# Attention loop of a windowed-attention and Fourier encoder: products in 64 rows of the TensorE array, two side by side

## The chip, the cores and the metric

One core of a Trainium2 chip runs the whole program. The metric is the device time of one execution in microseconds. Five engines work beside each other, each through its own queue of instructions: TensorE (PE: matrix products out of SBUF into the eight banks of PSUM), VectorE (DVE), ScalarE (ACT), GpSimd (POOL) and SyncE (SP, which here only issues DMAs). They meet at semaphores. A product of TensorE can use all 128 rows of its array (128 values of the summed dimension) or one half of them, rows 0 to 63 or 64 to 127; two products in different halves can run at the same time.

## The reference, cut to what matters

Two sequences (2048 and 512 tokens, 1024 channels) go through an attention layer and a Fourier layer. The change is in the attention layer, which is, for 16 query heads of 64 channels and 4 key heads, in blocks of 128 queries against up to 384 keys:

```python
h = rmsnorm(x, g)
z = h @ w_in                              # q, k, v, gate
scores = q . k * 64**-0.5 + bias          # a block and its two neighbours
m = max(scores, sink)
p = exp(scores - m)
p = p / (sum(p) + exp(sink - m))
o = p @ v
x = x + (o * silu(gate)) @ w_out
```

All matrix products have operands split into a high and a low part, so that each is three products: high x high, high x low, low x high (`matmul3`, line 114).

## The kernel before

**Chunks, turns, units.** The tokens are worked on in five chunks of 512 (line 37): chunk 0 is the short sequence, chunks 1 to 4 the long one. For a chunk, keys and values are projected first (`kv_proj`), then a loop of 17 turns (n = 0 to 16) does the attention: turn n computes scores and probabilities of one pair of heads for two blocks of queries (`new`, called `one` and `two`), and transposes and value products of those of the turn before (`old`). A block on the edge of a sequence has two key blocks (256 wide), the others three (384 wide): in chunk 0 one of each two blocks is narrow, in chunks 1 and 4 one of each four.

**What fills TensorE.** Into the turns the projections of q and gate of later head pairs are laid, and at the end those of the output. One unit is one step of 128 summed channels: three products of 512 columns, 8 units to a projection. A fixed list of quotas says how many units stand before and behind the value products, about four each.

**A turn on the engines.** TensorE: scores of both blocks (`scores`, L530), in 64 rows, since a head has 64 channels, the two heads side by side; transposes of the probabilities of the turn before (`transp`, L589), also in 64 rows; four units (L117) in 128 rows; value products (`av`, L615) in 128 rows; four units. VectorE adds the bias to the scores and takes the minimum of the negated ones (`biased`, L549), ScalarE takes the exponentials (`exps`, L557), VectorE inverts the sums and divides (`divide`, L565 and L569; one of four divisions on ScalarE, L567). `parts` (L597, L598) splits the transposed probabilities: ScalarE casts the high part out of PSUM, VectorE subtracts for the low one. `out_evac` takes the values out: copy `t2` on ScalarE (L624), two adds on VectorE (L633), then the gate on GpSimd and another split. `evac_q` and `evac_g` take a finished projection out (L465, L466; L473, L475), in chunk 0 with a scaling on VectorE ahead.

**Order.** Each engine works in the order in which the program is written (`seq` and `pe` chain the instructions), and waits where a semaphore is not there yet. Bias rows and weights come by DMA issued from SP; in chunk 0 the weights are split into high and low there (`load_w`, a cast of 1024 columns on ScalarE, four subtractions on GpSimd). `extra` lays side work into the turns: squares for the norms of the next chunk (L193) and sums and splits of the next layer's weights (L722, L778).

**PSUM.** Four banks (`psum`, buffers taken in turn by projections, transposes and value products) and four for scores (`spt`), of which the transposes of the second block also use one.

## Time and profile before

| | us |
|---|---|
| median of three runs | 1571.45 (1568.65 to 1572.51) |
| span of the profiled execution | 1566.4 |
| attention loop, chunk 0, window 41.3 to 174 | 132.4 TensorE busy of 132.7 |
| attention loop, chunk 2, window 459 to 603 | 144.0 TensorE busy of 144.0; VectorE 115.7, ScalarE 102.3, GpSimd 43.6 |

The span runs from the first to the last instruction that the profiler saw. "Busy" counts a product from its start to its modelled end; products overlap in the array, so that a TensorE that is always busy can still lose time between them, and the distance from start to start tells what a product really takes. In a group row the columns are line, engine, operation, output and inputs, shape, count, then busy time, mean ns of one, and idle time before them with what ended it. In a timeline row they are start and length in us, then the same; idle time before it stands in brackets. Of `64*128` and `128*128` the first number is the rows of the array.

### The profile page before, as it was taken

The numbers are of one execution on the slowest core, as the hardware profiler recorded it, in microseconds if no ns is written. First come the engines' busy times: TensorE is split into PE (matmuls) and PEld (weight loads), VectorE is DVE, ScalarE is ACT, GpSimd is POOL, SyncE is SP. The second block draws the span as 40 slices with busy tenths as digits, with TensorE's granted clock in tenths as the row PEclk, the third lists the DMA queues.
The fourth block names the chain that finished last, engine by engine and source line by source line (L and its number), as shares of the span: only waits on it lengthen the run. The fifth ranks groups of instructions, "written<-read, shape, count | busy, mean of one in ns | idle before, by whom it ended". The sixth has DMA issues, their size and how long they took to land.

```text
span 1566.4 us, 27701 instructions
## 1 busy us (share of the span) xinstructions
PE 1555.5 (99%) x9818; PEld 1306.6 (83%) x9818; DVE 1178.3 (75%) x2843; ACT 877.1 (56%) x2120; POOL 446.7 (29%) x614
## 2 busy tenths in 40 slices
PE   9999999999999999999999999999999999999998
PEld 7888888888898888988888888888888888888886
DVE  5888555887548886378873588767999888989886
ACT  7788534676237774256761476636556564333353
POOL 2575642421403413124224142123121211101100
PEclk9999999999999999999999999999999999999999
DMA  8588696665865576756749665675675569656852
GB/s 295 203 330 297 222 369 208 214 242 202 294 228 196 207 267 231 245 190 234 267 150 322 239 235 196 227 258 203 217 249 189 195 243 399 210 202 250 296 193 95
DMA packets 100423, 372.34 MB, mean 238 GB/s; under 512 B 11204, under 2 KB 22220, under 8 KB 82877
## 3 DMA queue, kind: packets, MB, share of 16 engines
q1 hardware_dynamic: 82716, 297.38, 54.2%
q0 software_dynamic: 16400, 70.04, 11.5%
q10 hardware_dynamic: 1168, 3.15, 0.6%
q8 instruction: 78, 1.28, 0.3%
q14 instruction: 61, 0.49, 0.1%
HBM read 280.06 MB, written 90.47 MB: 237 GB/s over the span
## 4 chain that ended last, share of the span: by engine, by line
PE 92%; DVE 3%; issue 2%; DMA 1%; POOL 0%; ACT 0%; SPq 0%; POOLq 0%; DVEq 0%; ACTq 0%
PE gp L117 15%; PE qp L117 14%; PE spt L117 11%; PE op L117 7%; PE av L615 6%; PE spt L530 6%; PE W L117 5%; PE fo L117 5%; PE vp L117 3%; PE Wo L117 3%; PE Z L117 3%; PE pt L589 3%; PE Zo L117 2%; PE z L1166 2%; PE ABp L117 1%
## 5 line engine op out<-in xcount | busy, mean ns | idle before, releaser
L117 PE MATMUL gp<-h,wg 128*128 128x512 f32 x960 | 237.8, 396 | 0.0
L117 PE MATMUL qp<-h,wq 128*128 128x512 f32 x960 | 237.1, 396 | 0.0
L549 DVE CUSTOM_DVE_ANT_0 S<-spt,b 128x385 f32<-128x385 f32 (+1 forms) x320 | 161.0, 529 | 98.9 <-PE spt L530 62.4
L117 PEld LDWEIGHTS gp<-h,wg 128*128 128x128 f32 x960 | 174.9, 188 | 37.3 <-issue 1.0
L117 PEld LDWEIGHTS qp<-h,wq 128*128 128x128 f32 x960 | 174.9, 188 | 36.5 <-issue 0.3
L557 ACT ACTIVATE S<-S 128x385 f32<-128x385 f32 (+1 forms) x320 | 190.7, 610 | 15.7 <-DVE S L549 15.7
L597 ACT CAST pts<-pt 128x384 fp32r<-128x384 f32 (+1 forms) x240 | 95.1, 462 | 179.3 <-PE pt L589 176.5
L598 DVE TENSOR_TENSOR pts<-pt,pts 128x384 fp32r<-128x384 f32 (+1 forms) x240 | 112.5, 519 | 22.4 <-ACT pts L597 22.2
L639 POOL TENSOR_TENSOR uT<-o,uT 128x256 fp32r<-128x256 f32 x75 | 55.5, 740 | 234.2 <-ACT uT L638 234.1
L117 PE MATMUL spt<-wo,uT 128*128 128x512 f32 x480 | 120.3, 391 | 0.0
L117 PE MATMUL op<-wo,uT 128*128 128x512 f32 x480 | 118.9, 391 | 0.0
L615 PEld LDWEIGHTS av<-pts,v 128*128 128x128 f32 x576 | 101.4, 188 | 18.8
L615 PE MATMUL av<-pts,v 128*128 128x512 f32 (+1 forms) x576 | 115.7, 341 | 0.0
L117 PE MATMUL fo<-wo,tTu 128*128 128x512 f32 x480 | 115.0, 392 | 0.0
L569 DVE TENSOR_SCALAR S<-S 128x384 f32<-128x384 f32 (+1 forms) x192 | 103.2, 537 | 6.8
L117 PEld LDWEIGHTS op<-wo,uT 128*128 128x128 f32 x480 | 89.4, 188 | 18.5
L117 PEld LDWEIGHTS spt<-wo,uT 128*128 128x128 f32 x480 | 89.1, 188 | 18.3
L530 PE MATMUL spt<-kwin,qab 64*128 64x384 f32 (+1 forms) x960 | 104.1, 343 | 0.0
L117 PEld LDWEIGHTS fo<-wo,tTu 128*128 128x128 f32 x480 | 88.3, 188 | 17.3
L530 PEld LDWEIGHTS spt<-kwin,qab 64*128 64x128 f32 x960 | 75.5, 184 | 28.2 <-issue 25.0
L635 POOL TENSOR_TENSOR o<-o,s 128x256 f32<-128x256 f32 x75 | 55.1, 735 | 129.4 <-DVE o L633 128.6
L589 PEld LDWEIGHTS pt<-ident,S 64*128 64x128 f32 x1328 | 69.8, 138 | 4.4 <-issue 1.8
(342 smaller groups left out, 3207.3 us busy)
## 6 DMA issues: line engine op xcount, KB each, us to landing
wo<-wsd SPq DMA_DIRECT2D x32, 1024.0 KB, 6.5
wq<-wsd SPq DMA_DIRECT2D x31, 1024.0 KB, 7.7
wg<-wsd SPq DMA_DIRECT2D x31, 1024.0 KB, 6.3
x<-x1d SPq DMA_DIRECT2D x40, 512.0 KB, 3.5
b<-b21d SPq DMA_DIRECT2D x40, 512.0 KB, 4.6
b<-rowd SPq DMA_DIRECT2D x40, 384.0 KB, 4.4
xs<-in_x_dram SPq DMA_DIRECT2D x23, 512.0 KB, 6.6
s2d<-gt POOLq DMA_DIRECT2D x40, 256.0 KB, 4.3
```

The lines of the kernel that those rows point to most:

```text
L117: ins = pe(PE.matmul(out, a[i], b[j], start=start and i + j == 0, stop=stop and i == 1, skip_group_check=more))
L530: pe(PE.matmul(banks[j][:, 2 + k0 * P : 2 + k1 * P], res["q"][rows, qp, b * P : (b + 1) * P], kwin[g][rows, kp, b * P + k0 * P : b * P + k ...
L549: seq(DVE, DVE.tensor_tensor_reduce(out=s[:, e0:e1], in0=ps[:, 1 + e0 : 1 + e1], in1=st["bias"][:, j, 386 - e1 : 386 - e0][:, ::-1], scale ...
L557: last_exp[0] = seq(ACT, ACT.activation(s[:, e0:e1], s[:, e0:e1], AF.Exp, bias=s[:, 386:387], scale=-1.0, accum_out=s[:, 387:388]))
L569: seq(DVE, DVE.tensor_scalar(s[:, ks], s[:, ks], den, None, ALU.mult))
L589: pe(PE.transpose(ps[h][:, kb, j, :], ss[j][rows, 1 + kb * P : 1 + (kb + 1) * P], ident[rows, rows]))
L597: seq(ACT, ACT.copy(hi, ps[:, k0:k1]))
L598: seq(DVE, DVE.tensor_tensor(lo, ps[:, k0:k1], f32(hi), ALU.subtract))
L615: pe(PE.matmul(to, v, pt, start=n == part == 0, stop=part == 1 and n in (1, len(todo) - 1), skip_group_check=n > 1,))
L635: eng.tensor_tensor(o, o, s, ALU.mult)
L639: low = eng.tensor_tensor(lo, o, f32(hi), ALU.subtract)
L1166: PE.matmul(to, m[part][:, g * P : (g + 1) * P], ch[:, 0, :, odd * P : (odd + 1) * P], start=part == 0, stop=part == 1,)
```

## The change

Every projection and score bank is now a PSUM tile with a fixed place: four for projections (`pj`), two for scores (`spt`), and two (`tv`) that transposes and value products share. In the loop every unit is laid beside a unit of another projection (`beside`): the one takes rows 0 to 63 of its operands, the other rows 64 to 127 of its own, and later the halves change places. The value products of two blocks run side by side in the same way, in two halves with a unit between them. Where a bank is to be written from the other half of the array, TensorE first waits until its last product into that bank is done (`swapped`). The turn is written anew: scores of the second block stand behind both transposes, and the values of a turn are taken out behind the first scores of the next. The transposes that spread the norms of the next chunk are in 64 rows too. Outside the loop projections stay whole (`whole`). The columns of all products together stay the same.

```diff
-    banks = [pstack.enter_context(tc.tile_pool(name="psum", bufs=4, space=PSUM))]
+    banks = []
+    psum = pstack.enter_context(tc.tile_pool(name="psum", bufs=1, space=PSUM))
+    pj = [psum.tile([P, 512], F32, name=f"pj{i}") for i in range(4)]
+    spsum = pstack.enter_context(tc.tile_pool(name="spsum", bufs=1, space=PSUM))
+    spt = [spsum.tile([P, 512], F32, name=f"spt{i}") for i in range(2)]
+    tv = spsum.tile([P, 2, 512], F32, name="tv")
+    spt += [tv[:, 0], tv[:, 1]]
...
+            class Product:
+
+                def __init__(self, place, left, right):
+                    self.ps, self.left, self.right, self.done, self.last = place, left, right, 0, [None, None]
...
+                def whole(self, k):
+                    first = self.done == 0
+                    self.done += 6
+                    matmul3(self.ps, self.left(k), self.right(k), first, self.done == 6 * KD, True)
...
+            def beside(*pairs):
+
+                swapped([(unit[0].last, h) for pair in pairs for h, unit in enumerate(pair) if unit is not None])
+                for upper, lower in pairs:
+                    both = []
+                    for h, unit in enumerate((upper, lower)):
+                        if unit is not None:
+                            both.append((unit[0], h) + unit[0].parts(unit[1], slice(64 * h, 64 * h + 64)))
+                    for i, j in ((0, 0), (0, 1), (1, 0)):
+                        for out, h, a, b in both:
+                            out.last[h] = pe(PE.matmul(out.ps, a[i], b[j], **out.flags()))
+
+            def swapped(places):
+
+                before = []
+                for last, h in places:
+                    if last[1 - h] is not None:
+                        before.append(last[1 - h])
+                        last[1 - h] = None
+                if before:
+                    wait = pe(PE.nop())
+                    for ins in before:
+                        tc.add_manual_dep(wait.ins, ins.ins.name, DONE, reason="other rows of a bank")
...
+                    products, last = [], [[None, None], [None, None]]
+                    for i in range(2):
+                        gb, k0, k1 = span(b + i)
+                        for kb in range(k0, k1):
+                            v = vblk[gb - 1 + kb][:, g].rearrange("p a d -> p (a d)")
+                            for part in range(2):
+                                pt = pts[:, part, i, kb].rearrange("p h q -> p (h q)")
+                                products.append((i, v, pt))
+                    by_block = [[m for m in products if m[0] == i] for i in range(2)]
+
+                    def half(swap):
+                        todo = by_block[::-1] if swap else by_block
+                        if swap:
+                            swapped([(last[1], 0), (last[0], 1)])
+                        for n in range(max(map(len, todo))):
+                            for h in range(2):
+                                if n < len(todo[h]):
+                                    i, v, pt = todo[h][n]
+                                    rows = slice(64 * h, 64 * h + 64)
+                                    last[i][h] = pe(PE.matmul(
+                                        tv[:, i, :256], v[rows], pt[rows], start=not swap and n == 0,
+                                        stop=swap and n == len(todo[h]) - 1, skip_group_check=True,
+                                    ))
...
-                    work += steps
+                fetches, loads, o, evacs = zip(*(qg_proj(c, i, hs, res[i // 2], invb0) for i in range(16)))
+                load_op, op_tiles, op = out_proj(c, uTs)
+                loads += tuple(lambda m=m: load_op(0, m) for m in range(4))
...
+                for k in range(KD):
+                    o[0].whole(k)
+                evacs[0]()
+                loads[2]()
+                loads[3]()
+                loads[4]()
+                for k in range(4):
+                    o[1].whole(k)
+                four = range(4)
...
+                def fills(n):
+
+                    t0, t1, t2, t3 = op_tiles
+                    if n < 14:
+                        x, y, z = (o + (t3,))[n + 1 : n + 4]
+                        return [((y, k), (x, 4 + k)) for k in four], [((y, 4 + k), (z, k)) for k in four]
...
+                    first, second = fills(n)
+                    if n == 0:
+                        beside(*(((o[1], 4 + k), (o[2], k)) for k in four))
                     if new:
...
-                        new[0].scores(one, spt[:2])
-                        if c:
-                            new[0].scores(two, spt[2:])
+                        new[0].scores(one)
+                    split = out_evac() if out_evac else None
+                    if new:
                         for j in range(2):
                             new[0].biased(one, j)
+                        new[0].exps(one, 0)
+                    beside(*first[:1])
                     if old:
                         old[0].transp(older[0], 0)
-                    if new and not c:
-                        new[0].scores(two, spt[2:])
+                        old[0].parts(older[0])
+                    if new:
+                        new[0].exps(one, 1)
...
+                    beside(*first[1:])
+                    if new:
+                        new[0].divide(one, 0, False)
+                        new[0].divide(one, 1, on_act == one)
...
-                    ahead_j = 2 if n == 15 else 1 if c and old else 0
                     if new:
-                        for j in range(ahead_j):
-                            new[0].biased(two, j)
+                        new[0].scores(two)
...
+                    if n < 15:
+                        evacs[n + 1]()
+                        loads[n + 5]()
                     if old:
-                        for b in older:
-                            old[0].parts(b)
+                        old[0].parts(older[1])
                     if new:
                         for j in range(2):
-                            new[0].exps(one, j)
-                    if split and c:
-                        split()
-                        split = None
...
-                        for j in range(ahead_j, 2):
                             new[0].biased(two, j)
...
-                        new[0].divide(one, 0, False)
...
-                        new[0].divide(one, 1, on_act == one)
...
-                    for i in range(quota[2 * n] if n < 15 else 18 - n):
-                        (work or op).pop(0)()
...
+                    beside(*second[:2])
                     if old:
-                        old[0].av(old[1])
-                        split = old[0].out_evac(old[1])
+                        halves = old[0].av(old[1])
+                        halves[0]()
+                    beside(*second[2:3])
+                    if old:
+                        halves[1]()
+                        out_evac = lambda old=old: old[0].out_evac(old[1])
+                    beside(*second[3:])
...
+                out_evac()()
```

**TensorE around the value products** (chunk 2, head pair 3; `q`/`g` for the projections of pair 4, `pts` the split probabilities). Before: four units, the value products, the next projection.

```order
L117 MATMUL qp2_4_6395<-h2_6_5138,wq2_4_6154 128x512 x3
L117 MATMUL qp2_4_6395<-h2_7_5146,wq2_4_6154 128x512 x3
L615 MATMUL av2_3_0_6497<-pts2_3_0_6428,v1_4_3036 128x512 x2
L615 MATMUL av2_3_0_6497<-pts2_3_0_6428,v2_5_5500 128x512 x2
L615 MATMUL av2_3_0_6497<-pts2_3_0_6428,v1_3_3008 128x256 x2
L615 MATMUL av2_3_0_6497<-pts2_3_0_6428,v2_6_5503 128x256 x2
L117 MATMUL gp2_4_6515<-h2_0_5088,wg2_4_6156 128x512 x3
L117 MATMUL gp2_4_6515<-h2_1_5097,wg2_4_6156 128x512 x3
```

Now: the last of six pairs of the first half, one unit of two projections side by side, and the first of the second half.

```order
L661 MATMUL tv_81<-pts2_3_0_7878,v2_6_6687 128x256
L661 MATMUL tv_81<-pts2_3_0_7878,v2_5_6684 128x256
L661 MATMUL tv_81<-pts2_3_0_7878,v2_6_6687 128x256
L484 MATMUL pj1_73<-h2_6_6311,wg2_4_7453 128x512
L484 MATMUL pj2_74<-h2_2_6278,wq2_5_7613 128x512
L484 MATMUL pj1_73<-h2_6_6311,wg2_4_7453 128x512
L484 MATMUL pj2_74<-h2_2_6278,wq2_5_7613 128x512
L484 MATMUL pj1_73<-h2_6_6311,wg2_4_7453 128x512
L484 MATMUL pj2_74<-h2_2_6278,wq2_5_7613 128x512
L661 MATMUL tv_81<-pts2_3_0_7878,v1_4_3618 128x256
L661 MATMUL tv_81<-pts2_3_0_7878,v1_3_3591 128x256
L661 MATMUL tv_81<-pts2_3_0_7878,v1_4_3618 128x256
```

The value products went from eight in 128 rows to two halves of 64 rows, with a unit between them.

**ScalarE, one turn** (head pair 4, first two blocks `S2_4_0` and `S2_4_1`; `t22_3_0` and `uT2_3` are values of pair 3, `th2_4` a gate). Before, from one copy `t2` to the next:

```order
L624 COPY t22_3_0_6506<-av2_3_0_6497 64x512
L510 COPY b2_4_6282<-sk_308 128x2x2
L597 CAST pts2_3_2_6547<-pt2_3_2_0_6548 128x6x64
L597 CAST pts2_3_2_6547<-pt2_3_2_1_6549 128x6x64
L597 CAST pts2_3_2_6547<-pt2_3_3_0_6562 128x6x64
L597 CAST pts2_3_2_6547<-spt0_233 128x6x64
L557 ACTIVATE S2_4_0_0_6543<-S2_4_0_0_6543 128x385
L557 ACTIVATE S2_4_0_1_6545<-S2_4_0_1_6545 128x385
L638 CAST uT2_3_6031<-o2_3_0_6508 128x256
L557 ACTIVATE S2_4_1_0_6575<-S2_4_1_0_6575 128x385
L557 ACTIVATE S2_4_1_1_6589<-S2_4_1_1_6589 128x385
L567 ACTIVATE S2_4_0_1_6545<-S2_4_0_1_6545 128x384
```

Now, the same stretch:

```order
L672 COPY t22_3_0_8018<-tv_81 64x512
L598 ACTIVATE S2_4_0_0_8024<-S2_4_0_0_8024 128x385
L636 CAST pts2_3_2_8036<-tv_81 128x6x64 x2
L598 ACTIVATE S2_4_0_1_8026<-S2_4_0_1_8026 128x385
L685 CAST uT2_3_7364<-o2_3_0_8020 128x256
L608 ACTIVATE S2_4_0_1_8026<-S2_4_0_1_8026 128x384
L527 ACTIVATE th2_4_8096<-pj1_73 128x512
L636 CAST pts2_3_2_8036<-tv_81 128x6x64 x2
L598 ACTIVATE S2_4_1_0_8106<-S2_4_1_0_8106 128x385
L598 ACTIVATE S2_4_1_1_8108<-S2_4_1_1_8108 128x385
```

The casts of the transposes stood together ahead of all exponentials; now the first two stand behind the first exponential, and the last two behind a division and the evacuation of a projection.

**VectorE, the same turn** from the adds of the values on. Before:

```order
L633 TENSOR_TENSOR o2_3_0_6508<-av2_3_0_6497,t22_3_0_6506 64x256 x2
L549 ISA S2_4_0_0_6543<-spt0_233,b2_4_6282 128x385
L549 ISA S2_4_0_0_6543 128x1
L549 ISA S2_4_0_1_6545<-spt1_234,b2_4_6282 128x385
L549 ISA S2_4_0_1_6545 128x1
L549 ISA S2_4_1_0_6575<-spt2_235,b2_4_6282 128x385
L549 ISA S2_4_1_0_6575 128x1
L598 TENSOR_TENSOR pts2_3_2_6547<-pt2_3_2_0_6548,pts2_3_2_6547 128x6x64
L598 TENSOR_TENSOR pts2_3_2_6547<-pt2_3_2_1_6549,pts2_3_2_6547 128x6x64
L598 TENSOR_TENSOR pts2_3_2_6547<-pt2_3_3_0_6562,pts2_3_2_6547 128x6x64
L598 TENSOR_TENSOR pts2_3_2_6547<-spt0_233,pts2_3_2_6547 128x6x64
```

Now:

```order
L680 TENSOR_TENSOR o2_3_0_8020<-tv_81,t22_3_0_8018 64x256 x2
L590 ISA S2_4_0_0_8024<-spt0_79,b2_4_7689 128x385
L590 ISA S2_4_0_0_8024 128x1
L590 ISA S2_4_0_1_8026<-spt1_80,b2_4_7689 128x385
L590 ISA S2_4_0_1_8026 128x1
L637 TENSOR_TENSOR pts2_3_2_8036<-tv_81,pts2_3_2_8036 128x6x64 x2
L606 RECIPROCAL S2_4_0_0_8024<-S2_4_0_0_8024 128x1
L610 TENSOR_SCALAR S2_4_0_0_8024<-S2_4_0_0_8024 128x384
L606 RECIPROCAL S2_4_0_1_8026<-S2_4_0_1_8026 128x1
L529 SCALAR_TENSOR_TENSOR s2_4_8098<-th2_4_8096,pj1_73 128x512
L637 TENSOR_TENSOR pts2_3_2_8036<-tv_81,pts2_3_2_8036 128x6x64 x2
```

The four subtractions (`pts`) stood together behind three biased scores; now two stand behind two biased scores, and the other two behind reciprocals, a division and the evacuation of the gate.

More of the change, by code (lines that the diff above doesn't have):

```diff
@@ L330, in bias_rows @@
                 return rowd, sk
-            spt = []
-            for i in range(4):
-                spt.append(spsum.tile([P, 512], F32, name=f"spt{i}"))
             def zeros(s):
@@ L381, in cols @@
                     return h[0][:, c0 : c0 + n], h[1][:, c0 : c0 + n]
-                kps = [spt[1 + t][:, :n] for t in range(2)]
+                kps = [(pj if c else spt)[1 + t][:, :n] for t in range(2)]
                 for k in range(KD):
@@ L410, in kv_proj @@
                     group = blocks[i0 : i0 + 4]
-                    ps = [bank(f"vp{c}_{i0}_{i}")[:, :256] for i in range(1 if norms else 0, len(group))]
                     if norms:
-                        ps.insert(0, spt[3][:, :256])
+                        ps = [t[:, :256] for t in spt[3:] + pj[1:]]
+                    else:
+                        ps = [t[:, :256] for t in (pj[2:3] if i0 else spt)]
                     for k in range(KD):
@@ L476, in evac_g @@
                     res["s"] = s
[L478 to L488 removed]
+                return fetch, load, out, evac_g if i % 2 else evac_q
             def attention(c, p, res, uTs):
@@ L536, in scores @@
                             ))
-                    for j in range(2):
-                        st["ps", b, j] = banks[j]
                 def edges(b):
```

215 lines of the change are left out of this document (94 added, 121 removed).

## The prediction

> **What bounds the kernel now.** First the page's busy times and its chain of work that ended last.
>
> ```profile
> PE 1555.5 (99%) x9818; PEld 1306.6 (83%) x9818; DVE 1178.3 (75%) x2843; ACT 877.1 (56%) x2120; POOL 446.7 (29%) x614
> PE 92%; DVE 3%; issue 2%; DMA 1%; POOL 0%; ACT 0%; SPq 0%; POOLq 0%; DVEq 0%; ACTq 0%
> ```
>
> TensorE works 99% of the span and carries 92% of the chain; VectorE and ScalarE have room on average. So I read TensorE's timeline of the attention loop next (chunk 2, two turns; a row is start, length, engine, line, tile, count).
>
> ```profile
> 502.71 1.33 PE L530 MATMUL spt<-kwin,qab 64*128 64x384 f32 x12
> 503.88 0.58 PE L589 MATMUL pt<-ident,S 64*128 64x64 f32 x13
> ...
> 504.71 3.03 PE L117 MATMUL qp<-h,wq 128*128 128x512 f32 x12
> 507.57 1.54 PE L615 MATMUL av<-pts,v 128*128 128x512 f32 x8
> 508.95 2.91 PE L117 MATMUL gp<-h,wg 128*128 128x512 f32 x12
> 511.79 1.33 PE L530 MATMUL spt<-kwin,qab 64*128 64x384 f32 x12
> ...
> 520.94 1.32 PE L530 MATMUL spt<-kwin,qab 64*128 64x384 f32 x12
> ```
>
> From score block to score block a turn takes 9.08 and 9.15 us, 9.12 on average. The rows follow each other without a hole: here TensorE waits for nobody. For the price of a product I take the output projection, where only 128-row products run.
>
> ```profile
> 405.67 2.88 PE L117 MATMUL op<-wo,uT 128*128 128x512 f32 x12
> 408.39 0.84 PE L117 MATMUL spt<-wo,uT 128*128 128x512 f32 x3
> ```
>
> Twelve take 2.72 us from start to start, 0.227 each. In the loop the twelve before the scores take 2.84 (508.95 to 511.79) and the twelve behind the transposes 2.86 (504.71 to 507.57): 0.12 and 0.14 more. The scores take 1.17 for six pairs; at 384/512 of 0.227 a pair they would take 1.02: 0.15 more. So one visit to the 64-row form costs **0.41 us**, and a turn is 8.71 us of work plus that.
>
> **The change, part by part.**
>
> *Visits removed.* With every product, transpose and value product of the loop in 64 rows, a chunk has one visit where it had 17 (turns 0 to 16): 16 x 5 chunks x 0.41 = 33 us less, if nothing else stopped TensorE.
>
> *Pairs in place of whole products.* A pair of 64-row products has the columns of one whole product. Not in the trace at 512 wide; nearest are the score pairs, 1.17/6 = 0.195 with both drains, 0.170 without, exactly the whole product's rate. Bounds: 0.227 (full overlap) and 0.454 (none, 24 x 0.227 = 5.4 us more a turn). I take 0.227, the rate of the score pairs; the far end contradicts that row and stays out of the range. The value product becomes 12 pairs of 256 columns. Before it was four of 512 and four of 256 in 1.38 us (507.57 to 508.95): 1.38 - 4 x 0.227 = 0.47, 0.118 for one of 256, and 12 x 0.118 = 1.41. No difference worth a term.
>
> *Two new waits of TensorE on itself in a turn* (before a bank takes products of the other rows). Between the product waited for and the wait stand six score products (0.51 us) or six projection products (0.68). Bounds: nothing, and a drain like that above, 0.2 each. I take nothing, since the work between outlasts one whole product:
>
> ```profile
> L117 PE MATMUL qp<-h,wq 128*128 128x512 f32 x960 | 237.1, 396 | 0.0
> ```
>
> 0.40 us from its start to its end; the rest is a rival below.
>
> *The moved hand-overs.* This decides. Transposes and value products now share two banks, and the values are copied out only after the next turn's first scores. By the changed order ScalarE runs: copy t, exp, two casts, exp, cast uT, division, evacuation of q or g, two casts, two exps; VectorE: two adds, two biased scores, two subtractions, reciprocal, division, reciprocal, evacuation, two subtractions, then the second block. The first value product stands behind the last subtraction, and the next copy t behind the last value product: a closed circle, once a turn. Its operations, in the trace before:
>
> ```profile
> 513.52 1.25 ACT L597 CAST pts<-pt 128x384 fp32r<-128x384 f32 x3 [3.02 <-PE pt L589]
> 514.64 0.51 ACT L597 CAST pts<-spt 128x384 fp32r<-128x384 f32 x1
> 515.01 0.65 ACT L557 ACTIVATE S<-S 128x385 f32<-128x385 f32 x1
> ...
> 515.62 0.64 ACT L557 ACTIVATE S<-S 128x385 f32<-128x385 f32 x1
> ...
> 517.82 0.61 ACT L567 ACTIVATE S<-S 128x384 f32<-128x384 f32 x1
> 518.33 0.58 ACT L473 ACTIVATE th<-gp 128x512 f32<-128x512 f32 x1
> 518.93 0.58 ACT L624 COPY t<-av 64x512 f32<-64x512 f32 x1
> ```
>
> ```profile
> 514.28 0.55 DVE L549 CUSTOM_DVE_ANT_0 S<-spt,b 128x385 f32<-128x385 f32 x1
> 514.76 0.08 DVE L549 DVE_READ_ACCUMULATOR2_ANT S<- 128x1 f32 x1
> 514.76 1.48 DVE L598 TENSOR_TENSOR pts<-pt,pts 128x384 fp32r<-128x384 f32 x3
> 516.16 0.54 DVE L598 TENSOR_TENSOR pts<-spt,pts 128x384 fp32r<-128x384 f32 x1
> ...
> 517.10 0.15 DVE L565 RECIPROCAL S<-S 128x1 f32<-128x1 f32 x1
> 517.28 0.42 DVE L569 TENSOR_SCALAR S<-S 128x384 f32<-128x384 f32 x1
> 517.62 0.22 DVE L565 RECIPROCAL S<-S 128x1 f32<-128x1 f32 x2
> ...
> 519.01 0.69 DVE L475 SCALAR_TENSOR_TENSOR s<-th,gp 128x512 f32<-128x512 f32 x1 [0.19 <-ACT th L473]
> 519.62 0.85 DVE L633 TENSOR_TENSOR o<-av,t 64x256 f32<-64x256 f32 x2
> ```
>
> An operation followed by one of its own engine is priced from start to start, one that is waited for by its length. Copy t 0.58; two adds 0.85; biased score 0.48 and its read 0.08; exp 0.61 (515.01 to 515.62); cast 0.51; two subtractions 0.47 each (a third of 514.76 to 516.16); reciprocal 0.18; division 0.34 (517.28 to 517.62); reciprocal 0.15; division on ScalarE 0.51; evacuation 0.58 there and 0.61 on VectorE; subtractions 0.47 and 0.54. Sum 7.43. Hand-overs: ScalarE to VectorE shows 0.10 (518.91 to 519.01) and occurs so twice where two semaphores are waited for; six more I estimate at 0.05: 0.50. TensorE from there: weights of the first pair 0.12 (as after a visit), six pairs 0.71, three projection pairs 0.68, five pairs 0.59 and the last one's length, 0.28 by the group of 256-wide value products:
>
> ```profile
> L615 PE MATMUL av<-pts,v 128*128 128x256 f32 x52 | 8.3, 282 | 0.0
> ```
>
> 2.38 in all. **The circle is 10.3 us**, longer than the 8.71 of work: TensorE idles 1.6 us a turn, mainly ahead of the value products, and a turn grows by 10.3 - 9.12 = 1.2. Ends: 10.1 with hand-overs of 0.03; 10.7 when the division runs 0.76 as it does beside GpSimd. Before, the casts and subtractions had no exp, division or evacuation between them, so no such circle filled a turn.
>
> *The other chunks.* In chunks 1 and 4 every other turn has a 256-wide first block, and the turn is shorter (two turns between these rows, 8.85 each):
>
> ```profile
> 265.59 1.14 PE L530 MATMUL spt<-kwin,qab 64*128 64x256 f32 x12
> 283.27 1.15 PE L530 MATMUL spt<-kwin,qab 64*128 64x256 f32 x12
> ```
>
> Narrow biased scores, exps, casts and subtractions are some 0.13 shorter each,
>
> ```profile
> L549 DVE CUSTOM_DVE_ANT_0 S<-spt,b 128x385 f32<-128x385 f32 x25 | 12.9, 552 | 0.0
> L549 DVE CUSTOM_DVE_ANT_0 S<-spt,b 128x257 f32<-128x257 f32 x24 | 9.3, 425 | 4.1 <-PE spt L530 2.5 <-issue 0.5 <-ACT b L510 0.4
> ```
>
> and three of them stand in an average circle: 9.9, +1.05. In chunk 0 six are narrow, but the cast of the next weights now stands between ScalarE's division and evacuation:
>
> ```profile
> 98.97 0.65 ACT L597 CAST pts<-pt 128x256 fp32r<-128x256 f32 x2 [1.39 <-PE pt L589]
> 99.50 1.06 ACT L145 CAST wq<-w32q 128x1024 fp32r<-128x1024 f32 x1
> 100.45 0.49 ACT L597 CAST pts<-pt 128x384 fp32r<-128x384 f32 x1
> ...
> 107.54 0.65 ACT L597 CAST pts<-pt 128x256 fp32r<-128x256 f32 x2
> ```
>
> 10.3 - 0.8 + 0.95 = 10.45, against 8.57 (98.97 to 107.54): +1.9.
>
> *Sum over 14 turns a chunk (1 to 14):* 14 x 1.9 + 28 x 1.05 + 28 x 1.2 = 27 + 29 + 34 = 90. Turn 0 has no values and turn 15 no evacuation (1.2 less, about even). Turn 16 has transposes and values with only six projection pairs: the value product's end, copy and adds (0.28 + 0.05 + 0.58 + 0.10 + 0.85 + 0.05 + 0.12 = 2.0) have two pairs of units, 1.4, beside them; casts and subtractions of a block (0.20 + 0.37 + 0.51 + 0.05 + 0.54 + 0.17 = 1.85, where 0.20 ends the transposes and 0.17 restarts TensorE) have 0.68 beside the first block and 1.36 beside the second. That stops TensorE 0.6 + 1.2 + 0.5 = 2.3 us, less the drains 1.9: 9 over five chunks. Squares (1.06 us) and splits of the next layer's weights (1.14 for two) now precede copy t on ScalarE:
>
> ```profile
> L193 ACT ACTIVATE xs<-xs 128x1024 f32<-128x1024 f32 x5 | 5.3, 1055 | 0.0
> ```
>
> ScalarE ends its second exp some 0.7 before copy t is due, so two squares in a turn cost 1.4, one 0.35, two splits 0.4. Chunks 1 to 3 have five squares (two, two and one to a turn), chunks 1 to 4 three turns with two splits: 3 x 3.2 + 12 x 0.4 = 15. Weights are fetched one at a time, two turns ahead: nothing. The Fourier phase is unchanged. Total 90 + 9 + 15 = 114 us, for a span of 1566.4 + 114 = 1680; the median, 1571.45, lies 5 us above the span: **1685**.
>
> **The rivals.**
>
> *Faster: the hand-overs stay hidden.* If ScalarE and VectorE delivered within TensorE's 8.71 us, only the drains would count: 1571 - 33 = **1538**. It decides at a circle of 8.7, 1.6 below the rows' sum; it needs an engine to take a ready operation ahead of a waiting one. For it speaks that both engines' sums (VectorE 75%) fit the turn; against it that each link is a measured length in one queue. [...]
>
> *No change: drains come back as waits.* If each self-wait cost 0.2, 2 x 0.2 x 80 = 32 would return the 33: **1571**, with the circle hidden. [...]
>
> *Half hidden:* a circle of 9.5 (0.8 less than the sum) would give 75 turns x 0.4 and the 9: about **1610**.
>
> **How the numbers follow.** Forecast 0.83; half hidden 0.05; no change 0.03; faster 0.09. The forecast's own range: below, 70 turns x 0.2 (the circle at 10.1), no cost of squares and splits (15) and none of turn 16 (9) make 1647, and as much again as the 0.2 for links shorter than their means 1633; above, 70 x 0.4 (the division beside GpSimd) and some 12 for chunk 0's fuller ScalarE make 1725. With 1630 to 1725 about 0.8 is inside, so no other case has to be. 0.3% is about what a measurement of this kernel can tell from no change. Faster 0.09, same 0.03, slower 0.88.
>
> **What would show it.** TensorE's timeline: turns of 10.3 us in chunks 2 and 3; a hole of 1 to 1.6 us ahead of the first value product, released by VectorE's subtraction; TensorE's busy share down to some 93%; no 0.12 gap between scores, transposes and projections; pairs at 0.227. Wrong if turns are near 8.7, if the holes stand at the self-waits, or if pairs take far more than 0.23.

## The result, and the profile after

| | before | after |
|---|---|---|
| median of the runs | 1571.6 us (1568.7 to 1572.5) | 1816.4 us (1811.6 to 1820.1) |
| span of the profiled execution | 1566.4 us | 1814.5 us |
| a quiet turn of chunk 2 (no square, split or transfer delays it) | 9.12 us | 11.66 us (the first two 11.51) |

The change makes the kernel slower by a ratio of 1.1563 (95% interval 1.1541 to 1.1586): 245 us where 113 were forecast. The direction was right, the size was less than half of it. The page of after, busy times and chain:

```profile
PE 1608.7 (89%) x13123; PEld 1333.5 (73%) x13123; DVE 1193.3 (66%) x2823; ACT 912.9 (50%) x2120; POOL 444.3 (24%) x614
...
PE 38%; DVE 24%; ACT 19%; issue 6%; DMA 5%; POOL 2%; SPq 0%; DVEq 0%; POOLq 0%; ACTq 0%
```

TensorE carried 92% of the chain and carries 38% now; VectorE and ScalarE work little longer than before (1193 and 913 us against 1178 and 877), but 43% of the chain runs through them. They are not full; they are waited for. TensorE's timeline of a turn of chunk 2 (projections left out) shows where:

```profile
620.47 0.68 PE L574 MATMUL spt<-kwin,qab 64*128 64x384 f32 x6
621.70 0.55 PE L627 MATMUL tv<-ident,S 64*128 64x64 f32 x12
625.11 0.59 PE L627 MATMUL tv<-ident,S 64*128 64x64 f32 x12 [0.74 <-DVE pts L637]
625.51 0.78 PE L574 MATMUL spt<-kwin,qab 64*128 64x384 f32 x6
629.21 0.97 PE L661 MATMUL tv<-pts,v 64*128 64x256 f32 x12 [1.53 <-DVE pts L637]
630.72 0.88 PE L661 MATMUL tv<-pts,v 64*128 64x256 f32 x12
632.13 0.34 PE L574 MATMUL spt<-kwin,qab 64*128 64x384 f32 x2
```

The turn takes 632.13 - 620.47 = 11.66 us, and the hole forecast ahead of the first value product is there (1.53 us, released by VectorE's subtraction). A second one, 0.74, stands ahead of the second transposes, released by the same line. ScalarE's and VectorE's casts and subtractions of this turn:

```profile
622.88 0.48 ACT L636 CAST pts<-tv 128x384 fp32r<-128x384 f32 x1
623.99 0.48 ACT L636 CAST pts<-tv 128x384 fp32r<-128x384 f32 x1 [0.62 <-DVE pts L637]
...
626.69 0.47 ACT L636 CAST pts<-tv 128x384 fp32r<-128x384 f32 x1
628.08 0.48 ACT L636 CAST pts<-tv 128x384 fp32r<-128x384 f32 x1 [0.92 <-DVE pts L637]
```

```profile
623.40 0.56 DVE L637 TENSOR_TENSOR pts<-tv,pts 128x384 fp32r<-128x384 f32 x1 [0.73 <-ACT pts L636]
624.50 0.56 DVE L637 TENSOR_TENSOR pts<-tv,pts 128x384 fp32r<-128x384 f32 x1 [0.55 <-ACT pts L636]
...
627.50 0.55 DVE L637 TENSOR_TENSOR pts<-tv,pts 128x384 fp32r<-128x384 f32 x1
628.60 0.56 DVE L637 TENSOR_TENSOR pts<-tv,pts 128x384 fp32r<-128x384 f32 x1 [0.55 <-ACT pts L636]
```

Read the two together: cast, subtraction, cast, subtraction, each waiting for the other engine. The second cast of a block, whose bank TensorE had filled by 622.25 (621.70 + 0.55), is released by the subtraction of the first head (0.62 and 0.92 us idle). In the sum of the prediction the second cast ran beside the first subtraction, as it did before. The groups over the whole kernel say the same:

```profile
L637 DVE TENSOR_TENSOR pts<-tv,pts 128x384 fp32r<-128x384 f32 (+1 forms) x320 | 169.3, 529 | 144.3 <-ACT pts L636 144.3
L661 PE MATMUL tv<-pts,v 64*128 64x256 f32 x1792 | 155.5, 296 | 114.1 <-DVE pts L637 114.1
...
L636 ACT CAST pts<-tv 128x384 fp32r<-128x384 f32 (+1 forms) x320 | 145.9, 456 | 126.6 <-DVE pts L637 115.3
```

The program has this wait in it. These are the casts of one turn in ScalarE's order with what they wait for, two blocks of two heads, first of after, then of the experiment "one link" below, in which the second head has another bank:

```
L636 CAST pts_3_2_8036<-tv 128x6x64 [waits PE_49,Activation_49]
L636 CAST pts_3_2_8036<-tv 128x6x64 [waits DVE_49]
L636 CAST pts_3_2_8036<-tv 128x6x64 [waits PE_49]
L636 CAST pts_3_2_8036<-tv 128x6x64 [waits DVE_49]
```

```
L636 CAST pts_3_2_8036<-tv 128x6x64 [waits PE_49,Activation_49]
L636 CAST pts_3_2_8036<-pj_72 128x6x64 [waits PE_49]
L636 CAST pts_3_2_8036<-tv 128x6x64 [waits PE_49]
L636 CAST pts_3_2_8036<-pj_72 128x6x64 [waits PE_49]
```

In after both heads' transposes lie in two banks of one tile (`tv`), and ScalarE's read of the second bank is ordered behind VectorE's read of the first. The traces agree: there the second cast of a block idles 0.62 and 0.92 us for VectorE, in "one link" it starts 0.38 behind the first (593.86 to 594.24) with no wait.

### The profile page after: what moved, and what is told of

It is laid out like the page before. It is cut to its first block, busy times and chain, and to the rows that moved or that the text cites. A ratio compares the mean times of both kernels' runs of the same rounds, so it can differ in the third digit from the quotient of the medians.

```text
span 1814.5 us, 34001 instructions
## 1 busy us (share of the span) xinstructions
PE 1608.7 (89%) x13123; PEld 1333.5 (73%) x13123; DVE 1193.3 (66%) x2823; ACT 912.9 (50%) x2120; POOL 444.3 (24%) x614
## 4 chain that ended last, share of the span: by engine, by line
PE 38%; DVE 24%; ACT 19%; issue 6%; DMA 5%; POOL 2%; SPq 0%; DVEq 0%; POOLq 0%; ACTq 0%
DVE pts L637 8%; ACT pts L636 6%; PE pj L124 5%; PE W L124 4%; ACT S L598 4%; PE pj L484 3%; PE tv L661 3%; PE spt L124 3%; DVE S L590 3%; PE tv L124 3%; PE Wo L124 3%; DVE o L680 3%; PE fo L124 2%; PE Z L124 2%; ACT t L672 2%
## 5 line engine op out<-in xcount | busy, mean ns | idle before, releaser
L484 PE MATMUL pj<-h,wg 64*128 64x512 f32 x1800 | 490.8, 402 | 0.0
L484 PE MATMUL pj<-h,wq 64*128 64x512 f32 x1680 | 455.8, 400 | 0.0
L484 PEld LDWEIGHTS pj<-h,wg 64*128 64x128 f32 x1800 | 324.5, 190 | 19.1 <-issue 1.8
L484 PEld LDWEIGHTS pj<-h,wq 64*128 64x128 f32 x1680 | 301.5, 189 | 17.7
L637 DVE TENSOR_TENSOR pts<-tv,pts 128x384 fp32r<-128x384 f32 (+1 forms) x320 | 169.3, 529 | 144.3 <-ACT pts L636 144.3
L661 PE MATMUL tv<-pts,v 64*128 64x256 f32 x1792 | 155.5, 296 | 114.1 <-DVE pts L637 114.1
L661 PEld LDWEIGHTS tv<-pts,v 64*128 64x128 f32 x1792 | 136.8, 194 | 155.6 <-DVE pts L637 148.6
L636 ACT CAST pts<-tv 128x384 fp32r<-128x384 f32 (+1 forms) x320 | 145.9, 456 | 126.6 <-DVE pts L637 115.3
L627 PE MATMUL tv<-ident,S 64*128 64x64 f32 x1792 | 90.0, 231 | 75.7 <-DVE pts L637 38.9
L484 PE MATMUL pj<-wo,uT 64*128 64x512 f32 x660 | 111.8, 402 | 0.0
```

Source lines behind the costliest of these rows:

```text
L484: out.last[h] = pe(PE.matmul(out.ps, a[i], b[j], **out.flags()))
L627: pe(PE.transpose(ps[h][:, kb, j, :], ss[j][rows, 1 + kb * P : 1 + (kb + 1) * P], ident[rows, rows]))
L636: seq(ACT, ACT.copy(hi, ps[:, k0:k1]))
L637: seq(DVE, DVE.tensor_tensor(lo, ps[:, k0:k1], f32(hi), ALU.subtract))
L661: last[i][h] = pe(PE.matmul(tv[:, i, :256], v[rows], pt[rows], start=not swap and n == 0, stop=swap and n == len(todo[h]) - 1, skip_group_ ...
```

## The experiments

Theory T: a turn is one closed circle of hand-overs between the three engines, as forecast, with one link more than the sum had. Rivals: R1, the 64-row products and TensorE's waits on itself; R2, the place of evacuation and weight load in the queues. Theory D came later, for chunk 0.

**Two tiles.** The shared tile becomes two, so the copy of the values is cut in two and the adds in four.

```diff
-    tv = spsum.tile([P, 2, 512], F32, name="tv")
+    tv = [spsum.tile([P, 512], F32, name=f"tv{i}") for i in range(2)]
...
-                    last_evac[0] = seq(ACT, ACT.copy(t2, ps[64:128]))
+                    for i in range(2):
+                        last_evac[0] = seq(ACT, ACT.copy(t2[:, i], ps[i][64:128]))
```

> The two banks for transposes and values become two tiles of one bank each; the copy of the values becomes two copies, the two adds four. Theory T (a turn is one closed circle of hand-overs between ScalarE, VectorE and TensorE, in which the second cast of a block also waits for the first subtraction because both read one tile): a cast and two hand-overs, some 0.65 us, leave the circle twice a turn, the extra copy and adds put 0.4 back: turns of chunk 2 from 11.66 to about 10.7, casts wait for TensorE only, time about 1745. Rival R1 (the 64-row products and TensorE's waits on itself cost the time): no change or a little more, 1816 to 1830. Rival R2 (the time comes from the evacuation of the projections and the weight casts standing between the two blocks in the queues): no gain either, 1816 to 1830.

Measured 1736.1 us (one run); quiet turns of chunk 2 mostly 10.49. Both are near T's numbers (1745 and 10.7), and both rivals fall.

**Evacuation late, and both edits together.**

```diff
+                    if old:
+                        old[0].parts(older[1])
                     if n < 15:
                         evacs[n + 1]()
                         loads[n + 5]()
-                    if old:
-                        old[0].parts(older[1])
```

> The evacuation of the next projection and the load of weights stand behind the casts and subtractions of the second block, nothing else is changed. Theory T: 0.58 on ScalarE and 0.61 on VectorE leave the circle: turns of chunk 2 from 11.66 to about 10.4; in chunk 0 the weight cast (1.05) and the scaling (0.69) leave it as well, 2.9 a turn at most; time about 1705. The interlock of the casts stays in view (each second cast released by VectorE's subtraction). Rival R1 (TensorE's own side): 1816. Rival R2 (it is the place of these steps and nothing else): turns near 9.1 and a time near 1580.

> Both edits: two tiles of one bank each, and evacuation and loads behind the second block's casts and subtractions. Theory T: the gains add, as both leave one circle: 11.66 - 0.9 - 1.2 = 9.5 a turn in chunk 2, time about 1640. If only one of the two carries the time (R2), it is that of the better one alone. Rival R1: 1816.

Measured 1799.3 and 1719.0 us (one run each): a gain of 17 where T expected 110, and the same 17 on top of the two tiles. Both expectations miss. In the first kernel quiet turns became mostly 10.94, 0.7 shorter and not 1.2, and the turns with splits did not change (11.96). The end of a turn of that kernel, ScalarE's rows (without its short reads of the accumulator):

```profile
649.24 0.60 ACT L519 ACTIVATE qab<-pj 128x512 fp32r<-128x512 f32 x1
651.08 0.62 ACT L598 ACTIVATE S<-S 128x385 f32<-128x385 f32 x1 [1.23 <-DVE S L590]
651.69 0.60 ACT L598 ACTIVATE S<-S 128x385 f32<-128x385 f32 x1
652.29 0.18 ACT L554 COPY b<-sk 128x4 f32<-128x4 f32 x1
652.50 0.58 ACT L672 COPY t<-tv 64x512 f32<-64x512 f32 x1
```

Copy t no longer waits for TensorE, as it does in quiet turns of after (0.57 to 0.66 us); it stands right behind the exponentials of the second block, which wait for biased scores that now stand behind the evacuation. So the step left one circle and lengthened another through the same two engines, and in that one the splits count in full (11.96 - 10.94 = 1.02, against 0.31 in after). This is read from the rows; no kernel tests it alone.

**No casts.** Without casts and subtractions the kernel shows TensorE's own pace.

```diff
-                        st["pts"] = ap.tile([P, 2, 2, 3, 2, P], F32R, align_bytes=LINE, tag="pt", bufs=1, name=f"pts{c}_{p}_{b}")
+                        st["pts"] = fixed[0]
...
-                    for h in range(2):
+                    for h in ():
```

> The casts and subtractions of the transposed probabilities are left out; the value products read a buffer that is filled once per chunk. TensorE does all its work, with the same 64-row products and waits on itself. Theory T: the circle is open, TensorE sets the pace: turns of chunk 2 about 8.7, a share of TensorE of 97% or more, time about 1540 (33 below the kernel before: the visits to the 64-row form that are gone). Rival R1: TensorE's side costs the time, so turns stay above 10 and the time above 1700.

Measured 1633.9 us (one run), between T's 1540 and the 1700 of R1, so the total decides nothing; the turns do. The score blocks of chunk 2:

```profile
588.50 0.76 PE L576 MATMUL spt<-kwin,qab 64*128 64x384 f32 x5
...
597.35 0.80 PE L576 MATMUL spt<-kwin,qab 64*128 64x384 f32 x6
...
606.26 0.76 PE L576 MATMUL spt<-kwin,qab 64*128 64x384 f32 x5
```

588.50 to 606.26 is two turns, 8.88 each, with the same pairs and the same waits of TensorE on itself. R1 is out. The rest of the total is chunk 0: it takes 266 us against 209 before (three turns of 19 to 21 us, see the theory on chunk 0) and starts 4 us later, behind the filling of the buffer. Chunks 1 to 4 together are 4 us above before, so the gain that T had put in its 1540 is not there either.

**One link.** The cleanest form: no instruction more or less, the second head's transposes go into the projection bank that is free in the turn.

```diff
+                    other = pj[n % 4][:, :384] if n < 16 else spt[1][:, 2:386]
...
-                    ps = [tv[:, h, :384].rearrange("p (k j q) -> p k j q", k=3, j=2) for h in range(2)]
+                    ps = st["pt"] = [t.rearrange("p (k j q) -> p k j q", k=3, j=2) for t in (tv[:, 0, :384], other)]
```

> The changed kernel with one link taken away and no instruction more or less: the second head's transposes go into the projection bank that is free through the turn, so that the second cast of a block reads another tile than the first subtraction and waits for TensorE alone. Theory T (the sum of the circle was right but for this link, a cast and two hand-overs, 0.65 a block): quiet turns of chunk 2 from 11.66 to 10.3 to 10.4, time 1816 - 75 x 1.3 = about 1720. Rival (the gain of the two-tile kernel came from its finer copies and adds, which release the banks earlier): above 1770.

Measured 1720.9 us, ratio to before 1.0963 (1.0931 to 1.0994). ScalarE's first two casts of a turn of chunk 2, and VectorE's subtractions:

```profile
593.86 0.48 ACT L636 CAST pts<-tv 128x384 fp32r<-128x384 f32 x1
594.24 0.49 ACT L636 CAST pts<-pj 128x384 fp32r<-128x384 f32 x1
```

```profile
594.37 0.56 DVE L637 TENSOR_TENSOR pts<-tv,pts 128x384 fp32r<-128x384 f32 x1 [0.73 <-ACT pts L636]
594.85 0.55 DVE L637 TENSOR_TENSOR pts<-pj,pts 128x384 fp32r<-128x384 f32 x1
```

The second cast (594.24) runs beside the first subtraction (594.37), and the pair of subtractions has no gap. Quiet turns of this kernel take 10.1 to 10.25 us: the forecast's circle was 10.3. So the rival of finer copies and adds is out as well. By chunk, from its first score block to the next one's (the last: to the end of the span); the forecast's terms sorted by chunk:

| chunk | before | forecast more | after more | one link more |
|---|---|---|---|---|
| 0 | 208.7 | 28 | 77 | 61 |
| 1 | 209.4 | 21 | 43 | 24 |
| 2 | 213.1 | 23 | 47 | 24 |
| 3 | 207.1 | 23 | 47 | 29 |
| 4 and on | 686.8 | 18 | 34 | 16 |
| sum | | 113 | 248 | 154 |

The link costs 248 - 154 = 94 us, 70% of the miss of 135. Without it chunks 1 to 4 are at 93 against the 85 forecast, and chunk 0 holds the other 33.

**Chunk 0.** Waits of ScalarE in its loop, before and after, by line waited for:

```profile
ACT b L510 <- DMA b<-rowd: 1.0, 1, 1.0
ACT wq L145 <- DMA w32q<-in_w_in_dram: 0.3, 1, 0.3
```

```profile
ACT wq L152 <- DMA wsd<-wlate: 7.6, 2, 3.8
ACT b L554 <- DMA b<-rowd: 5.8, 1, 5.8
```

Two things stand in ScalarE's queue ahead of a copy of values until a transfer lands: a weight cast whose tile is held by the store of a late weight, and a copy of bias ends. With one link taken away, less covers them; in that kernel they are 13.1 and 7.1:

```profile
ACT wq L152 <- DMA wsd<-wlate: 13.1, 2, 6.6
ACT b L554 <- DMA b<-rowd: 7.1, 1, 7.1
```

The first attempt on them:

```diff
-LATE = (8, 9)
-AGAIN = (0, 10, 11, 12)
+LATE = ()
+AGAIN = (0, 8, 9, 10, 11, 12)
...
-                    load = SP.dma_start(
+                    load = (SP if c else POOL).dma_start(
```

> The changed kernel with two edits to chunk 0 alone: the two late weights are no longer converted inside its loop (chunk 1 converts them for itself), so that no weight tile is held by a store, and the bias rows are requested on GpSimd's queue instead of behind the weight fetches in SyncE's. Theory D (part of chunk 0's excess is ScalarE standing in its queue for a transfer: 7.6 us at weight casts behind the late weights' stores and 5.8 at a bias row): these waits go, chunk 0's loop shrinks by 10 to 20 us, chunk 1 pays 2 to 5, total near 1803. Rival (chunk 0 is longer through its scaling, weight cast and interlock alone, the transfers only fill waits that would be there anyway): chunk 0 within 4 us of before, total 1816 to 1821.

Measured 1822.0 us (one run; after took 1811.6 to 1820.1), so no gain. Chunk 0's loop was 10 us shorter (189.9 against 200.1 from its first to its last score block), but the stretch from there to chunk 1's first score block was 9 longer (95.0 against 85.9), as the conversions came back in it. The bias edit did not touch its wait: the row waited for is that of the next chunk's first pair. In before its copy stands behind a copy t, in after ahead of one. A second attempt pins that copy behind the loop and gives the late weights buffers of their own:

```diff
-                    elif not c:
-                        after(ends, last_inv[0])
+                    else:
+                        after(ends, last_evac[0] if c else last_inv[0])
...
+        if late:
+            w32 = fetch_w(n, name, late)
+            hi, lo = (xtile([P, D], F32R, f"w{name}{i}") for i in range(2))
```

> The changed kernel with only these edits: the two late weights of chunk 0 are converted in buffers of their own, earlier by a turn, so that no weight tile waits for their stores; and the next chunk's first copy of bias ends, which stood in ScalarE's queue ahead of a copy of values while its row was still in transfer, is issued behind the last copy of values. Theory D: ScalarE's waits for transfers in the loops go (7.6 + 5.8 us in chunk 0, 4.1 in chunk 1), at no cost between the loops: 1816 becomes 1798 to 1806, turns of chunk 2 stay at 11.65 and 11.97. Rival (the waits only fill time that the circle takes anyway): 1816.

Measured 1813.3 us (one run), within the range of after: no gain is shown where 10 to 18 were expected, and the total is the rival's. The bias wait went (the turn that had it fell from 15.76 to 11.12 in chunk 0 and from 15.45 to 11.25 in chunk 1), but the late weights only moved theirs: their casts now wait for their own fetches, and chunk 0 as a whole took 288 us against 286.

```profile
ACT wlate L142 <- DMA w32late<-in_w_in_dram: 11.7, 2, 6.4
ACT wg L162 <- DMA w32g<-in_w_in_dram: 6.8, 2, 6.1
```

So the waits that D names are there, and one could be taken away; that the time of the others can be had back is not shown.

**A version against both.** First block's transposes into the two free projection banks right behind the first scores, second block's into the shared tile, its two casts apart with an exponential between, all other steps behind the casts:

```diff
+                    if old:
+                        old[0].transp(older[0], 0, pt[:2])
+                        old[0].parts(older[0])
...
+                        old[0].transp(older[1], 1, pt[2:])
+                        old[0].parts(older[1], (0,))
+                    if new:
+                        new[0].exps(one, 1)
+                        new[0].divide(one, 0, False)
+                    if old:
+                        old[0].parts(older[1], (1,))
```

> A candidate against both. The first old block's transposes go into the two projection banks that are free in a turn, right behind the first scores; the second block's into the shared banks; its two casts stand apart with an exp and a division between them, so the second cast's wait for the first subtraction is covered; evacuation, weight load and second block stand behind all casts and subtractions. Theory T (the circle, not the 64-row products, costs the time): with each link started half a turn earlier TensorE sets the pace, turns of chunk 2 about 8.8 to 9.0, chunks 1 to 4 together some 10 us below the kernel before; chunk 0 keeps its transfer waits (about 30 us, as they are no longer covered): total 1570 to 1600. Rival R1 (64-row pairs or TensorE's waits on itself cost more than the visits): turns above 9.2 and the time above 1640 with TensorE busy throughout.

Measured 1650.4 us, ratio 1.0508 (1.0478 to 1.0539). Quiet turns of chunk 2 took 8.85 to 8.89 as T expects; the total is 50 above the upper end: chunk 0 had two turns of 22 us and one of 19, and turns with squares or splits took 9.2 to 10.7. The next kernel is this one with the edits of the first attempt on chunk 0.

> The previous candidate with the two edits to chunk 0. Theories T and D together: chunk 0 loses most of its transfer waits, 20 to 30 us less than the previous candidate: 1545 to 1575. If D is wrong, the same as the previous candidate.

Measured 1634.4 us: 16 less and not 20 to 30, and 60 above the range. Chunk 0's loop shrank by 26 us, the conversions ahead of chunk 1 took 10 back, and the bias wait (7.9) stayed, as it had with the same edits above. Then squares and splits behind copy t or behind the casts, with the edits of the second attempt:

```diff
                     split = out_evac() if out_evac else None
+                    if n < 15:
+                        extra(4 * n)
```

> The candidate with four banks, with the two edits against transfers, and with the squares and splits for the next stage behind the copy of values, or behind the casts, instead of ahead of the copy. Theories T and D: the stalled turns of chunk 0 (22 us, twice) fall to 9, the turns with squares or splits from 9.5 to 10.6 to about 9.0: 1650 - 27 - 10 - 5 x 4 = 1593, within 20. Rival (those turns are long for another reason, TensorE's own): above 1615.

Measured 1596.8 us, ratio 1.0168 (1.0130 to 1.0205), as expected, though not in chunk 0, where turns of 9.8 to 16.2 us remain. TensorE in two turns of chunk 2:

```profile
531.81 0.70 PE L581 MATMUL spt<-kwin,qab 64*128 64x384 f32 x6
533.72 0.88 PE L668 MATMUL tv<-pts,v 64*128 64x256 f32 x12
535.13 0.89 PE L668 MATMUL tv<-pts,v 64*128 64x256 f32 x12
536.54 0.70 PE L581 MATMUL spt<-kwin,qab 64*128 64x384 f32 x6
540.67 0.70 PE L581 MATMUL spt<-kwin,qab 64*128 64x384 f32 x6
...
549.55 0.70 PE L581 MATMUL spt<-kwin,qab 64*128 64x384 f32 x6
```

(549.55 - 531.81)/2 = 8.87 a turn, nothing waits, and the longest turns with squares take 9.1 and 9.2: turns of before take 9.12. The last kernel moved the late weights to the end of chunk 0's loop and a step of the output projection ahead of the last value products:

```diff
+                    if c == 0 and i in (55, 59):
+                        load_w(0, LATE[i == 59], f"late{i}", late=True, w32=late.pop())
...
-                    beside(*second[:2])
+                    beside(*second[: 3 if n == 16 else 2])
```

> The last candidate with the two late weights converted in the last turns of chunk 0, and in each chunk's last turn three steps of the output projection ahead of the value products instead of two. Theory D (chunk 0's remaining 28 us over the kernel before are mostly weight fetches that wait for buffers and share the queues with the late weights): chunk 0 some 12 us less, and 1 us per chunk from the last turn: 1597 - 17 = 1580, within 10. If chunk 0 is long for ScalarE's and VectorE's work instead: 1592.

Measured 1599.2 us where 1580 was expected: chunk 0's early turns fell to 8.9 to 9.4 (from 9.8 to 16.2), but one of 14 us stayed in its middle (14.2, before 14.1), and two near its end grew to 14. The waits moved with the weights. No kernel here beats the one before. The best of them (1596.8) is 25 us behind it: its chunk 0 takes 236.8 us against 208.7, and chunks 1 to 4 together 1 us less than before. How to load chunk 0's weights beside this order stays open.

## Why the prediction was right or wrong

- **Direction and mechanism: right.** TensorE waits in a closed circle that is longer than its work, and the hole stands ahead of the first value product. Its busy share fell to 89%, where 93% was forecast.
- **The sum of the circle: the step that failed.** "Its operations, in the trace before" counts the lengths of before and, with them, the order of before: a second cast that runs beside the first subtraction. The change puts both heads in one tile, and the second cast then waits for that subtraction. In the rows above the two subtractions of a block start 1.10 apart (623.40 to 624.50), without the link 0.48 (594.37 to 594.85). The 0.62 between are a cast (0.48), two hand-overs (0.07 together: VectorE idles 0.55 ahead of the second subtraction, and 0.48 of it is the cast) and the 0.07 by which the subtractions overlapped. Two blocks make 1.24 of the 11.66 - 10.24 = 1.42 a turn. Most of the rest is TensorE's: from the end of the last subtraction to that of the last value product it takes 2.45 us in after and 2.30 without the link, where a first pair of products starts ahead of that end. Over the whole kernel the link costs 94 us. The rest of the sum held: 10.24 without the link against 10.3, and no other step of that circle is off by more than 0.13 (an exponential 0.73 for 0.61, TensorE's part 2.25 for 2.38, which cancel). The order printed with the change names `tv` as the source of both casts and of both subtractions, so the sharing could be seen there.
- **"Weights are fetched one at a time, two turns ahead: nothing": wrong for chunk 0.** ScalarE waits there 13 us for transfers in after and 22 in the kernel without the link (13.1, 7.1 and 2.1 for a fetch), where the loop of before has 1.3. How much of chunk 0's 33 us they make is not shown: taken away in the changed kernel they gave nothing, in the one with four banks the same edits gave 16 us.
- **Squares and splits: right in size, short by a chunk.** In chunk 2 of after the turns with two squares take 13.0 and 13.2 against 11.66 (1.4 forecast), those with splits 11.97 (0.4 forecast, 0.31 measured). But chunk 0 has five squares too, and the sum gave it none: in the kernel without the link its turns with a square take 10.9 to 11.3, those without 10.1: 5 us over the five.
- **Visits removed, 33 us: half right.** TensorE's own pace is 8.88 a turn, not 8.71. These rows of the kernel of 1596.8 us show why (of each pair of projections only the product of `wg`; below, the last pair ahead of the second half of the value products):

```profile
538.17 0.55 PE L634 MATMUL tv<-ident,S 64*128 64x64 f32 x12
538.51 0.47 PE L491 MATMUL pj<-h,wg 64*128 64x512 f32 x1
538.83 0.39 PE L491 MATMUL pj<-h,wg 64*128 64x512 f32 x1
539.06 0.39 PE L491 MATMUL pj<-h,wg 64*128 64x512 f32 x1
...
543.76 0.39 PE L491 MATMUL pj<-h,wg 64*128 64x512 f32 x1
543.99 0.89 PE L668 MATMUL tv<-pts,v 64*128 64x256 f32 x12
```

  A pair of 512 columns takes 0.23 (0.231 on average), near the 0.227 of a whole product, but the first one behind each of the two transposes takes 0.31. So the pairs of a turn take 22 x 0.231 + 2 x 0.31 = 5.70 and not 24 x 0.227 = 5.45; the transposes give some of it back (0.34 each, 0.68 for both, where before they took 0.83). Of the 0.41 a turn 9.12 - 8.88 = 0.24 remains, 18 us of the 33. What the prediction calls a drain is the 0.12 to 0.15 us that rows of before take longer where the two forms meet; no run shows what the array does in it.
- **Waits of TensorE on itself cost nothing: right.** One stands ahead of the second half of the value products, and that half starts 0.23 behind the pair before it (543.76 to 543.99), as any pair does; between pairs of projections the only gaps are those behind the transposes. So the rival that let each cost 0.2 is out: the waits are over when they are reached.
- **One tile or two.** In after the second cast and the first subtraction of a block are ordered although they read two banks, because these are one tile, and the cast idles 0.62 and 0.92 us. In the kernel with one link less, a cast (594.24, 0.49 long) and a subtraction (594.37, 0.56 long) of two banks in two tiles run side by side, and are about as long as in after (0.48 and 0.56).

## What to carry to other kernels

Before lengths of the old trace are summed along a new chain, list for every instruction in it what it will wait for in the new program; an engine's read can wait for another engine's read when both are of one tile (here for 0.62 and 0.92 us in a turn). Give two engines that work in a relay a tile each (here worth 94 us). When an order is made tighter, look in each queue for what stands ahead of the critical step and waits for a transfer: it was covered before, and it is not any more (in chunk 0's loop ScalarE waits 13 us for transfers in after, 1.3 in before). And look where a step goes that is taken out of one circle: here the evacuation entered the next (17 us gained where 110 were expected).

## What the hardware showed that was not expected

TensorE's granted clock, 1.00 through the whole loop before, falls to 0.50 near most of the longest holes of chunk 0's loop in after. These rows of the stretches of after are the beginning of chunk 0's loop, 10 us around one of its waits for a transfer, and chunk 2 (length, then busy time of PE, PEld, DVE, ACT and POOL, clock, DMA share and GB/s):

```profile
41.00:103.00 62.00, 48.93 (x464) 41.10 (x462) 36.35 (x123) 32.95 (x81) 25.30 (x38) 0.88 0.52 190
...
116.00:126.00 10.00, 5.52 (x46) 4.56 (x46) 3.81 (x13) 4.39 (x10) 4.82 (x7) 0.66 0.85 319
...
580.00:760.00 180.00, 143.28 (x1628) 116.50 (x1624) 113.84 (x338) 105.42 (x265) 42.40 (x59) 1.00 0.46 164
```

In the first and the last TensorE's busy share is the same, 79% and 80%. In chunk 2 the holes are up to 1.9 us long, and the clock stays at 1.00. In the first stretch there are five holes of 2.1 to 3.0 us, each with some 3.4 us at a clock of 0.50 at its end or shortly behind it (57.0 to 60.4 is one), which makes 0.88. About a hole of 4.5 us, in the second, the clock is 0.50 for 6.8 us. Four other holes of 2.1 to 2.4 us (up to 112, 130, 154 and 192) have no such stretch. So holes of 2.1 to 3.0 us were enough here, though not always; what decides it is not shown. Over chunk 0's loop in after (201 us) the clock is 0.89 on average, so the lower clock can account for at most some 0.11 x 201 = 22 us of its excess, an estimate; no kernel separates this from the waits themselves.
